# A mixture-of-experts stage with 64 slots per expert, two experts side by side in the array, and float32 gate and up products on raw weights

## Chip, cores, metric

One core of one Trainium2 chip runs the whole program. The metric is the time of one execution in device microseconds (us), the median of several runs.

## What is computed

Two transformer blocks on 256 tokens of width 1024, all in float32. The change touches only the end of the second block, a two-level mixture of experts (4 groups of 4 experts, hidden width 256), and the norm that follows it:

```python
glog = xt @ w_rg + b_rg;  gsel = argmax(glog);  ggate = softmax(glog)[gsel]
elog_g = (xt @ w_re + b_re).reshape(-1, 4, 4)[gsel]      # the chosen group's experts
top_p, top_i = top_k(softmax(elog_g), 2);  top_p /= sum(top_p)
comb = one_hot(4 * gsel + top_i, 16) * (ggate * top_p)    # summed over the two
act = silu(xt @ w1[e]) * (xt @ w3[e]) * comb[:, e]        # gate, up; 1024 -> 256
y = sum over e of act @ w2[e]                             # down; 256 -> 1024
return rmsnorm(x + y)
```

So each token belongs to one group and uses two of that group's four experts. Routed with the reference's inputs of four seeds, the largest group has 83 tokens and the largest expert 54.

## The kernel before, in words

Weights are packed on the host into 134 chunks of 128 x 2048 float32 (1 MiB), in the order of use; the last 48 are the experts': three for each, two of gate and up (each with half of the 1024 input rows, 512 output columns: 256 of gate, 256 of up), one of down. `_emit` (L318) issues a chunk's load on SyncE's queue into a raw buffer and then splits it: ScalarE writes a rounded copy `whi` in the float32r type (L351), VectorE writes the remainder `wlo` (L352). A product in nearly full float32 precision is then three float32r products: hi by hi, hi by lo, lo by hi. The loads are issued in order, each when its raw buffer is free, so SyncE runs ahead as far as buffers allow; `chunk()` (L358) splits one chunk ahead of its use.

`moe_route` (L1689) forms router logits, picks each token's group (`oh`), and ranks the tokens of a group with a triangular product (`rank`); from these come one-hot matrices `Sg` that put the tokens of a group into 128 slots. `moe` (L1731) gathers groups 0 and 1 by a product with `Sg` and splits the result into `ghi`, `glo`; groups 2 and 3 come later by indirect DMA on GpSimd's queue and TensorE transposes. While the first expert is on TensorE, VectorE computes the weights of the experts (`eg`, `ex`, two calls of `first_max`). `facts` (L1807) brings each slot's token number and weights into slot order by small float32 products.

`experts` (L1851) then walks over the 16 experts. For each: 24 float32r products of 512 columns (`ahead`: gate and up for the 128 slots of the group), Silu and multiply (`act`), two transposes and a split (`turn`), and 12 products of 512 columns (`down`) that add to the group's `y`. After a group's fourth expert `finish` (L1928) adds the residual, normalizes, and scatters the rows to the output by indirect DMA. At the very end, a group with over 128 tokens would make a fallback run (L1976).

The list of who multiplies what with float32 operands matters for the change: `values2` (L757, through `pairs`, L746) already puts two products of 64 output rows side by side in the array, with plain float32 operands.

Of the kernel before, what the change touches and what calls it, by code (L numbers as in the profile page):

```python
# [7 lines left out]
F32 = mybir.dt.float32  # L8
# [9 lines left out]
N_CHUNKS = 134  # L18

# [82 lines left out]
def _pack(x):  # L102
# [81 lines left out]
    for e in range(18):  # L184
        if e < 16:
            w13 = np.concatenate([_rows(x["w_exp_gate_2"][0, e]), _rows(x["w_exp_up_2"][0, e])], 2)
            put(w13[:, 0:4])
            put(w13[:, 4:8])
        if e > 1:
            put(_rows(x["w_exp_down_2"][0, e - 2]))  # L190
# [66 lines left out]
class Kernel:  # L257
    def __init__(self, ctx, tc, ins, out, dump=None, stop=None):
# [13 lines left out]
        self.extra = None  # L272
# [20 lines left out]
    def big(self, tag, name, dt=F32):  # L293
        n, bufs = {"nt": (3072, 1), "m": (2048, 2), "rawm": (2048, 6)}[tag]
        return (self.sb if tag == "m" else self.mx).tile([128, n], dt, name=name, tag=tag, bufs=bufs)
# [22 lines left out]
    def _emit(self, i, cols, first=None):  # L318
# [3 lines left out]
        j = i - LATE - (i > EXTRA)  # L322
        tag = "raw" if j < 0 else None if i == EXTRA else RAW_LATE[j % len(RAW_LATE)]
        if tag is None and self.extra:
            raws, self.extra = self.extra, None
        else:
            if tag in (None, "raw"):
                raw = self.wp.tile([128, 2048], F32, name="raw", tag="raw", bufs=self.NRAW)
            else:
                raw = self.big(tag, "raw")  # L330
            raws = [raw[:, 0:1024], raw[:, 1024:2048]]
            if not first and i != 1:
                nc.sync.dma_start(raw[:, :cols], self.ins["W"][i, :, :cols])
        out, c = [], 0
        for step, load, then in first if first else [(1024, None, None)] * (cols // 1024):
# [4 lines left out]
            if c % 1024 == 0:  # L340
                if i >= LATE_M and (2 * i + c // 1024) % 3 == 2:
                    hl = self.big("m", "whilo", F32R)
                    hi, lo = hl[:, 0:1024], hl[:, 1024:2048]
                else:
                    hi = self.wp.tile([128, 1024], F32R, name="whi", tag="whi", bufs=self.NHI)
                    lo = self.wp.tile([128, 1024], F32R, name="wlo", tag="wlo", bufs=self.NHI)
                out.append((hi, lo))
# [1265 lines left out]
    def late_pool(self):  # L1613

        self.mx_ctx.close()
        self.mx = self.mx_ctx.enter_context(self.tc.tile_pool(name="mo", bufs=1))
        self.bufs.update(s=4, t2=2)

    def moe_start(self):
# [7 lines left out]
        self.wr = self.t("s", name="wr")[:, 0:160]  # L1627
# [7 lines left out]
        self.lg = self.t("s", name="lg")[:, 0:40].rearrange("p (a b) -> p a b", a=2)  # L1635

        self.meta = self.t("s", name="meta")[:, 0:48].rearrange("p (a b) -> p a b", a=2)
        nc.gpsimd.memset(self.meta, 1.0)
        nc.gpsimd.tensor_copy(self.meta[:, :, 0], self.con("tok"))
        self.oh = self.t("c", (2, 4), F32R, name="oh")  # L1640
        self.gm = self.t("c", (2, 1), name="gm")
        self.rank = self.t("c", (2, 4), name="rank")
        self.Sg = [self.t("t2", (2, 256), F32R, name="Sg") for _ in range(2)]
# [45 lines left out]
    def moe_route(self):  # L1689
# [28 lines left out]
        nc.vector.tensor_copy(self.rank, pr[:, 0:8].rearrange("p (a b) -> p a b", a=2))  # L1718
        def places(eng, gs):
            for h in range(2):  # L1720
                for gi in gs:
                    eng.tensor_scalar(self.Sg[gi // 2][:, h, 128 * (gi % 2):128 * (gi % 2) + 128], self.con("iota"),
                                      self.rank[:, h, gi:gi + 1], self.oh[:, h, gi:gi + 1].bitcast(F32),
                                      op0=ALU.is_equal, op1=ALU.mult)

        places(nc.vector, (0, 1))
        for i in range(2):
            self.turn_s(2 + i, tp[i])
        places(nc.gpsimd, (2, 3))

    def moe(self):  # L1731
        nc, x = self.nc, self.x
        con, par = self.con, self.par
        thi, tlo = self.thi, self.tlo
        meta = self.meta
        lg, oh, gm, rank, Sg = self.lg, self.oh.bitcast(F32), self.gm, self.rank, self.Sg
        first_max = self.first_max
# [9 lines left out]
        ghi = [self.t("a4", (4, 256), F32R, name="ghi") for _ in range(2)]  # L1747
        glo = [self.t("a4", (4, 256), F32R, name="glo") for _ in range(2)]
        gp = [self.ps("acc", (2, 256)) for _ in range(4)]
        for m, h in [(0, 0), (1, 0), (0, 1), (1, 1)] + [(m, h) for m in range(2, 8) for h in range(2)]:  # L1750
            c = slice(128 * m, 128 * m + 128)
            self.mm(gp[m // 2][:, m % 2], thi[h][:, c], Sg[0][:, h], h == 0 and m % 2 == 0, False,
                    skip_group_check=True)
            self.mm(gp[m // 2][:, m % 2], tlo[h][:, c], Sg[0][:, h], False, h == 1, skip_group_check=True)
        for m in range(8):
            self.split(ghi[m // 4][:, m % 4], glo[m // 4][:, m % 4], gp[m // 2][:, m % 2], par("n2", m))
        hg = [v[:, k] for v in ghi for k in range(4)], [v[:, k] for v in glo for k in range(4)]

        self.extra = [self.t("a4", name="raw") for _ in range(2)]
        for k in range(2):  # L1760
            nc.sync.dma_start(self.extra[k], self.ins["W"][EXTRA, :, 1024 * k:1024 * k + 1024])
# [3 lines left out]
        nc.vector.tensor_tensor(dg, gl, b4(gm), ALU.subtract)  # L1765
        nc.scalar.activation(dg, dg, AF.Exp)
        gs = c3("gs", 1)
        nc.vector.tensor_reduce(gs[:, :, 0], dg, axis=AX.X, op=ALU.add)
        nc.vector.reciprocal(gs, gs)

        eg = c3("eg")
        for gi in range(4):
            el = lg[:, :, 4 + 4 * gi:8 + 4 * gi]
            if gi == 0:
                nc.vector.tensor_tensor(eg, el, b4(oh[:, :, 0:1]), ALU.mult)
            else:
                tmp = c3("tmp")
                nc.vector.tensor_tensor(tmp, el, b4(oh[:, :, gi:gi + 1]), ALU.mult)
                nc.vector.tensor_tensor(eg, eg, tmp, ALU.add)
        em = c3("em", 1)  # L1780
        nc.vector.tensor_reduce(em[:, :, 0], eg, axis=AX.X, op=ALU.max)
        ex = c3("ex")
        nc.vector.tensor_tensor(ex, eg, b4(em), ALU.subtract)
        nc.scalar.activation(ex, ex, AF.Exp)
        warm = self.t("c", name="warm")[:, 0:1]
        nc.scalar.activation(warm, ex[:, 0, 0:1], AF.Silu)
        oh1, oh2 = c3("oh1"), c3("oh2")
        m1, m2 = c3("m1", 1), c3("m2", 1)
        first_max(oh1, ex, m1)
        rest = c3("rest")  # L1790
        nc.vector.scalar_tensor_tensor(rest, oh1, -2.0, ex, op0=ALU.mult, op1=ALU.add)
# [234 lines left out]
```

## Time and profile before

| | |
|---|---|
| runs | 802.88 us median of 3 (802.06 to 804.18) |
| the profiled execution | 801.04 us, span 799.2 us |
| TensorE busy | 770.2 us (96% of the span), 5640 matmuls |
| VectorE, ScalarE, GpSimd busy | 616.7, 452.8, 98.4 us |
| granted TensorE clock | 0.985 of full speed, mean |

The span runs from the first to the last instruction; the rest of the execution's time lies around it. Matmuls overlap in the pipeline: what one costs in a stream is the distance between the starts of two, not its duration.

### The profile page before, as it was taken

The numbers are of one execution on the slowest core, as the hardware profiler recorded it, in microseconds if no ns is written. First come the engines' busy times: TensorE is split into PE (matmuls) and PEld (weight loads), VectorE is DVE, ScalarE is ACT, GpSimd is POOL, SyncE is SP. The second block draws the span as 40 slices with busy tenths as digits, with TensorE's granted clock in tenths as the row PEclk, the third lists the DMA queues.
The fourth block names the chain that finished last, engine by engine and source line by source line (L and its number), as shares of the span: only waits on it lengthen the run. The fifth ranks groups of instructions, "written<-read, shape, count | busy, mean of one in ns | idle before, by whom it ended". The sixth has DMA issues, their size and how long they took to land. (4 is left out here: it accounts for less than half of the span.)

```text
span 799.2 us, 14325 instructions
## 1 busy us (share of the span) xinstructions
PE 770.2 (96%) x5640; PEld 711.2 (89%) x5640; DVE 616.7 (77%) x1163; ACT 452.8 (57%) x751; POOL 98.4 (12%) x99
## 2 busy tenths in 40 slices
PE   8999999999999999999999899999999899999994
PEld 8988889899999999999999779988899887877873
DVE  6677587777666767887877898777497689999995
ACT  7357346645544455755764233555465477888882
POOL 1000002000000000300100644200014412020111
PEclk9999999999999999999999979999999899999998
DMA  8754424555545455454333313431585759989910
GB/s 320 266 205 171 158 60 153 165 204 164 201 166 203 164 202 167 158 210 158 109 107 132 114 59 81 158 102 58 227 353 165 237 224 363 352 311 385 373 67 28
DMA packets 30505, 149.90 MB, mean 188 GB/s; under 512 B 9440, under 2 KB 10464, under 8 KB 13792
## 3 DMA queue, kind: packets, MB, share of 16 engines
q1 hardware_dynamic: 20880, 141.70, 49.9%
q10 hardware_dynamic: 8400, 4.08, 1.8%
q0 software_dynamic: 1152, 3.15, 1.0%
q8 instruction: 46, 0.75, 0.4%
q14 instruction: 27, 0.22, 0.1%
HBM read 146.42 MB, written 3.54 MB: 188 GB/s over the span
## 5 line engine op out<-in xcount | busy, mean ns | idle before, releaser
L352 DVE TENSOR_TENSOR wlo<-raw,whi 128x1024 fp32r<-128x1024 f32 (+1 forms) x237 | 293.6, 1246 | 88.1 <-ACT whi L351 86.0
L351 ACT ACTIVATE whi<-raw 128x1024 fp32r<-128x1024 f32 (+1 forms) x237 | 247.3, 1048 | 172.2 <-PE acc L368 85.8
L368 PE MATMUL acc<-hhi,whi 128*128 128x256 f32 x344 | 100.2, 291 | 0.0
L368 PE MATMUL acc<-hhi,wlo 128*128 128x256 f32 x344 | 99.2, 289 | 0.6 <-DVE wlo L352 0.6
L368 PE MATMUL sm<-hhi,whi 128*128 128x256 f32 x352 | 99.5, 283 | 0.0
L368 PE MATMUL sm<-hlo,whi 128*128 128x256 f32 x352 | 99.4, 282 | 0.0
L368 PE MATMUL sm<-hhi,wlo 128*128 128x256 f32 x352 | 99.0, 281 | 0.0
L368 PE MATMUL acc<-hlo,whi 128*128 128x256 f32 x344 | 98.6, 287 | 0.0
L368 PEld LDWEIGHTS acc<-hhi,wlo 128*128 128x128 f32 x344 | 65.8, 192 | 2.6 <-issue 1.6
L368 PEld LDWEIGHTS acc<-hhi,whi 128*128 128x128 f32 x344 | 65.9, 192 | 1.3 <-issue 0.8
L368 PEld LDWEIGHTS sm<-hhi,wlo 128*128 128x128 f32 x352 | 66.7, 189 | 0.0
L368 PEld LDWEIGHTS acc<-hlo,whi 128*128 128x128 f32 x344 | 65.9, 191 | 0.8 <-issue 0.6
L368 PEld LDWEIGHTS sm<-hlo,whi 128*128 128x128 f32 x352 | 66.2, 188 | 0.0
L368 PEld LDWEIGHTS sm<-hhi,whi 128*128 128x128 f32 x352 | 66.0, 188 | 0.0
L457 POOL TENSOR_TENSOR sqacc<-sqacc,sq 128x256 f32<-128x256 f32 x19 | 16.2, 851 | 331.4 <-ACT sq L456 330.6
L368 PE MATMUL acc<-alo,whi 128*128 128x256 f32 x176 | 49.5, 281 | 0.0
L368 PE MATMUL acc<-ahi,wlo 128*128 128x256 f32 x176 | 49.4, 281 | 0.0
L368 PE MATMUL acc<-ahi,whi 128*128 128x256 f32 x176 | 49.3, 281 | 0.0
L368 PE MATMUL acc<-xhi,wlo 128*128 128x256 f32 x160 | 45.7, 286 | 1.0 <-DVE wlo L352 0.8
L368 PE MATMUL acc<-xhi,whi 128*128 128x256 f32 x160 | 46.2, 289 | 0.0
L368 PE MATMUL acc<-xlo,whi 128*128 128x256 f32 x160 | 45.4, 284 | 0.0
L352 DVE TENSOR_TENSOR whilo<-raw,whilo 128x1024 fp32r<-128x1024 f32 x32 | 39.0, 1219 | 0.4
(504 smaller groups left out, 1888.6 us busy)
## 6 DMA issues: line engine op xcount, KB each, us to landing
raw<-in_W_dram SPq DMA_DIRECT2D x130, 1024.0 KB, 5.0
raw<-in_W_dram SPq DMA_DIRECT2D x5, 512.0 KB, 6.8
raw<-in_W_dram SPq DMA_DIRECT2D x4, 256.0 KB, 4.8
xd<-xr ACTq DMA_DIRECT2D x2, 512.0 KB, 8.2
dec<-in_con_dram ACTq DMA_DIRECT2D x2, 384.0 KB, 4.3
conm<-in_con_dram SPq DMA_DIRECT2D x1, 576.0 KB, 7.0
xa<-in_xT_dram SPq DMA_DIRECT2D x2, 256.0 KB, 4.4
xb<-in_xT_dram SPq DMA_DIRECT2D x2, 256.0 KB, 5.2
```

Of the source, the lines that this page charges most:

```text
L351: nc.scalar.activation(h, r, AF.Copy)
L352: nc.vector.tensor_tensor(l, r, h.bitcast(F32), ALU.subtract)
L368: return self.nc.tensor.matmul(out, a, b, start=start, stop=stop, **kw).ins
L457: (eng or nc.gpsimd).tensor_tensor(acc, acc, sq, ALU.add)
```

## The change

Each expert gets 64 slots of its own, and each two experts of a group form a pair that fills 128 slots. The input of a pair is one float32 tile `X` (1024 x 128 slots, not split). Gate and up of the two experts of a pair run as plain float32 products on the raw chunks, 64 slots each, into the two halves of one PSUM tile. Their chunks are no longer split; a raw buffer is held until TensorE has used it, and the ring of raw buffers grows from 9 to 11. After Silu, a float32 product with a one-hot matrix `E` turns the activations and spreads them from an expert's 64 slots to the group's 128 in one step, once for each expert, in place of the two transposes. Down is as before. The choice of the experts moves from `moe` into `moe_route`, ahead of the ranking. Two pairs' inputs come from the one-hot gather, the other six by indirect DMA and transposes. The fallback runs if a group has over 128 tokens or an expert over 64.

```diff
+MOE = []
+for _n in range(9):
+    MOE += [(_k, 2 * _n + _e) for _k in range(2) for _e in range(2)] if _n < 8 else []
+    MOE += [(2, 2 * _n - 2 + _e) for _e in range(2)] if _n else []
...
     def _emit(self, i, cols, first=None):
+            j = i - LATE
+            raw = self.big((["rawm"] * 6 + ["raw"] * 3 + ["m"] * 2 * (i >= MOE0))[j % 9 if i < MOE0 else (j - 8) % 11],
+                           "raw")
...
+        if i >= MOE0 and MOE[i - MOE0][0] < 2:
+            return raw
...
     def moe_route(self):
-            self.keep_warm(2, self.slt[:, 0], self.thi[0][:, 0:256])
+            self.keep_warm(6, self.slt[:, 0], self.thi[0][:, 0:256])
+        nc.vector.tensor_tensor(by, self.lg[:, :, 4:20].rearrange("p h (g j) -> p h j g", g=4), ohj, ALU.mult)
+        nc.vector.tensor_reduce(eg, by, axis=AX.X, op=ALU.add)
+        nc.vector.tensor_reduce(em[:, :, 0], eg, axis=AX.X, op=ALU.max)
+        nc.vector.tensor_tensor(ex, eg, em.to_broadcast([128, 2, 4]), ALU.subtract)
+        nc.scalar.activation(ex, ex, AF.Exp)
+        self.first_max(oh1, ex, self.m1)
+        nc.vector.scalar_tensor_tensor(rest, oh1, -2.0, ex, op0=ALU.mult, op1=ALU.add)
+        self.first_max(oh2, rest, self.m2)
+        nc.vector.tensor_tensor(sel, oh1, oh2, ALU.add)
+        nc.vector.tensor_tensor(self.oe..., sel..., ohg, ALU.mult)
-        self.mm(pr[:, 0:8], self.slt[:, 0], self.oh, True, False, skip_group_check=True)
-        ranked = self.mm(pr[:, 4:8], self.slt[:, 1], self.oh[:, 0], False, True, skip_group_check=True)
+        for p, v, n in ((pe, self.oe, 16), (pg, self.oh, 4)):
+            self.mm(p, self.slt[:, 0], v, True, False, skip_group_check=True)
+            ranked = self.mm(p[:, n:2 * n], self.slt[:, 1], v[:, 0], False, True, skip_group_check=True)
...
     def moe(self):
+        def rows(idx):                      # indirect DMA of 128 rows of x
+        def turned(row, dst):               # 8 transposes, 2 scaled copies by VectorE
...
+        def gate_up(n, amid):
+            p = self.ps("sm")
+            last = None
+            for k2 in range(2):
+                ch = self.chunk(), self.chunk()
+                for k in range(4):
+                    for e in range(2):
+                        r = slice(64 * e, 64 * e + 64)
+                        with self.tc.issue_after(last) if last else contextlib.nullcontext():
+                            last = mm(p[r], X[n][:, 4 * k2 + k, r], ch[e][:, 512 * k:512 * k + 512], k2 + k == 0,
+                                      k2 == 1 and k == 3, skip_group_check=True)
+                if k2 == 0:
+                    amid()
...
+        def act(n):
+            nc.scalar.activation(sl, p[:, 0:256], AF.Silu, scale=F.mt[:, n, 2:3])
+            nc.vector.scalar_tensor_tensor(a, p[:, 256:512], F.rc[:, n:n + 1], sl, op0=ALU.mult, op1=ALU.mult)
+            nc.gpsimd.tensor_scalar(E, con("iota"), F.place[:, n:n + 1], None, op0=ALU.is_equal)
+        def spread(n):
+            pts = [self.ps("sm", (2, 128)) for _ in range(2)]
+            self.pairs([[(pts[e][:, i], a[rr[e], 128 * i:128 * i + 128], E[rr[e]], True, True) for i in range(2)]
+                        for e in range(2)], skip_group_check=True)
...
+                self.split(ahi, alo, pts[e])
...
     def finish(...):
-                eng = nc.gpsimd if n else nc.vector
-                eng.tensor_tensor(o, o, fng[:, 512 * n:512 * n + 512], ALU.mult)
+                nc.vector.tensor_tensor(o, o, fng[:, 512 * n:512 * n + 512], ALU.mult)
...
+        for n in range(9):
+            if n < 8:
+                gate_up(n, (lambda: spread(n - 1)) if n else (lambda: None))
+            if n == 0:
+                pair_facts()                # 16 small float32 products, 8 pairs
+                for m in range(2, 4):
+                    prow[m] = rows(F.idx[:, 0, m:m + 1])
+                group_facts()               # 8 small float32 products, 4 groups
+            if n < 8:
+                act(n)
+            else:
+                spread(7)
+            if n % 2 == 0 and n < 8:
+                grow[n // 2] = rows(F.idg[:, 0, n // 2:n // 2 + 1])
+            if n and n + 3 < 8:
+                prow[n + 3] = rows(F.idx[:, 0, n + 3:n + 4])
+            if n:
+                prepare(n + 1)              # turned(prow[n + 1], X[n + 1])
+                down(n - 1)                 # 24 float32r products, split chunks
+                if n % 2 == 0:
+                    finish(y, grow[n // 2 - 1], scatter(n // 2 - 1))
...
-        with self.tc.If(reg > 128):          # reg: the largest group
+        with self.tc.If(reg > 128):          # reg: largest group, or twice the largest expert
```

## Rows read from the trace of the kernel before

**Rows 1.** The page's first line, of the whole execution.
```profile
span 799.2 us, 14325 instructions
```
**Rows 2.** Stretches: length, busy PE, PEld, DVE, ACT, POOL (count), clock, DMA share, GB/s.
```profile
636.50:643.60 7.10, 7.09 (x39) 6.85 (x40) 3.12 (x12) 2.17 (x6) 4.02 (x5) 0.63 0.90 290
643.60:788.40 144.80, 142.32 (x643) 114.12 (x642) 137.62 (x210) 114.35 (x153) 18.16 (x10) 1.00 0.74 278
```
**Rows 3.** TensorE in order of time, expert stage: start, length us, tiles, count.
```profile
658.23 0.39 PE L368 MATMUL sm<-whilo,ghi 128*128 128x512 f32 x1
658.46 1.86 PE L368 MATMUL acc<-meta,Sg 128*128 128x24 f32 x16
660.16 0.48 PE L368 MATMUL sm<-whilo,ghi 128*128 128x512 f32 x1
```
**Rows 4.** TensorE in order of time around one call of values2.
```profile
524.06 0.27 PE L368 MATMUL acc<-hlo,whi 128*128 128x256 f32 x1
524.37 0.87 PE L368 MATMUL sm<-pt,bV 128*64 128x256 f32 x8
525.17 0.93 PE L368 MATMUL sm<-bK,bq 64*128 64x128 f32 x8
```
**Rows 5.** The same around four calls of values2 in a row.
```profile
566.71 2.82 PE L368 MATMUL sm<-de,U 128*64 128x256 f32 x32
569.46 0.38 PE L368 MATMUL acc<-hhi,whi 128*128 128x256 f32 x1
```
**Rows 6.** TensorE groups by shape, 480 to 634 us: count, busy us, mean ns.
```profile
L368 PE MATMUL acc<-hhi,wlo 128*128 128x256 f32 x142 | 40.2, 284 | 0.6 <-DVE wlo L352 0.6
L368 PE MATMUL sm<-pt,bV 128*64 128x256 f32 x16 | 2.6, 404 | 0.0
```
**Rows 7.** TensorE in order of time: transposes of gathered rows.
```profile
675.33 0.60 PE L1844 MATMUL sm<-con,row 128*128 128x128 f32 x4
675.68 0.48 PE L368 MATMUL sm<-whi,ghi 128*128 128x512 f32 x1
```
**Rows 8.** TensorE in order of time, ranking; in brackets idle time, releaser.
```profile
636.51 0.59 PE L368 MATMUL sm<-oh,slt 128*128 128x8 f32 x2 [2.57 <-DVE oh L1687]
636.96 1.20 PE L368 MATMUL acc<-thi,slt 128*128 128x256 f32 x4
```
**Rows 9.** The expert choice, all engines in order of time.
```profile
646.51 0.17 DVE L1783 TENSOR_TENSOR ex<-eg,em 128x8 f32<-128x8 f32 x1
...
646.96 0.16 DVE L1681 TENSOR_REDUCE m<-ex 128x2 f32<-128x8 f32 x1 [0.27 <-ACT ex L1784]
```
**Rows 10.** VectorE in order of time: the choice of the second expert.
```profile
649.63 0.17 DVE L1687 TENSOR_TENSOR oh<-e,f 128x8 f32<-128x8 f32 x1
649.83 0.17 DVE L1791 SCALAR_TENSOR_TENSOR rest<-oh,ex 128x8 f32<-128x8 f32 x1
650.03 0.16 DVE L1681 TENSOR_REDUCE m<-rest 128x2 f32<-128x8 f32 x1
650.23 0.36 DVE L1684 SCALAR_TENSOR_TENSOR e<-rest,m,con 128x4 f32<-128x4 f32 x2
```
**Rows 11.** Tile raw, 640 to 800 us: count, duration ns min/median/max, starts; DMA landing.
```profile
L352 DVE TENSOR_TENSOR wlo<-raw,whi x60: 1204/1217/2354, 647.9 to 783.5; 128x1024 fp32r<-128x1024 f32 x60
L333 SPq DMA_DIRECT2D raw<-in_W_dram x35: 327/328/328, 651.7 to 756.8; - x35
...
DMA to landing us min/median/max: 4.7/7.0/8.5
```
**Rows 12.** A stretch with loads queued throughout; columns as in Rows 2.
```profile
720.00:735.00 15.00, 15.00 (x68) 12.13 (x67) 14.52 (x18) 12.58 (x18) 1.29 (x1) 1.00 1.00 412
```
**Rows 13.** The tail in order of time.
```profile
789.46 0.68 DVE L1937 TENSOR_TENSOR row<-row,fng 128x512 f32<-128x512 f32 x1
...
790.38 1.25 POOL L1937 TENSOR_TENSOR row<-row,fng 128x512 f32<-128x512 f32 x1 [10.37 <-ACT acc L1935]
```
**Rows 14.** Line L1824, the indirect row gathers: time to landing.
```profile
DMA to landing us min/median/max: 6.2/6.5/7.0
```

More of the change, by code (lines that the diff above doesn't have):

```diff
@@ L340, in _emit @@
             if c % 1024 == 0:
[L341 to L346, printed above, removed]
+                hi = self.wp.tile([128, 1024], F32R, name="whi", tag="whi", bufs=self.NHI)
+                lo = self.wp.tile([128, 1024], F32R, name="wlo", tag="wlo", bufs=self.NHI)
                 out.append((hi, lo))
@@ L1769, in moe @@
         nc.vector.reciprocal(gs, gs)
[L1771 to L1791, printed above, removed]
-        first_max(oh2, rest, m2)
         den = c3("den", 1)
-        nc.vector.tensor_tensor(den, m1, m2, ALU.add)
+        nc.vector.tensor_tensor(den, self.m1, self.m2, ALU.add)
         nc.vector.reciprocal(den, den)
@@ L1804, in moe @@
         fng = self.t("a4", name="fng")
         nc.scalar.dma_start(fng, self.ins["fng"])
[L1807 to L1817 removed]
+        pc = self.ps("sm", (20,))
@@ L1928, in finish, with down @@
-        def finish(y, fact):
-            _, _, idx, row = fact
+                self.split(ahi, alo, pts[e])
+                P[n].append((ahi, alo))
+        def down(n):
+            nonlocal y
+            if n % 2 == 0:
+                y = [self.ps("acc"), self.ps("acc")]
+            for e in range(2):
+                ahi, alo = P[n][e]
+                first, last = n % 2 + e == 0, n % 2 == 1 and e == 1
+                ch = self.chunk()
+                for k, c2 in ((0, 0), (1, 0), (0, 1), (1, 1)) if last else ((0, 0), (0, 1), (1, 0), (1, 1)):
+                    hi, lo = ch[k]
+                    c = slice(512 * c2, 512 * c2 + 512)
+                    mm(y[c2], ahi[:, k], hi[:, c], first and k == 0, False, skip_group_check=True)
+                    mm(y[c2], ahi[:, k], lo[:, c], False, False, skip_group_check=True)
+                    mm(y[c2], alo[:, k], hi[:, c], False, last and k == 1, skip_group_check=True)
@@ L1931, in finish @@
+        ends = []
+        def finish(y, row, store):
             ss = self.t("c", name="ss")[:, 0:2]
@@ L1941, in finish @@
             nc.vector.tensor_scalar(row[:, 0:624], row[:, 0:624], rr, None, op0=ALU.mult)
-            d = nc.gpsimd.indirect_dma_start(
-                out=self.out, out_offset=bass.IndirectOffsetOnAxis(ap=idx, axis=0), in_=row, in_offset=None,
-                bounds_check=S - 1, oob_is_err=False)
-            for other in ends:
-                self.tc.declare_no_dep(d.ins, other.ins, reason="rows of another group")
-            ends.append(d)
-        known = []
-        def fact(gi):
-            if not known:
-                known.extend(facts([[Sg[g // 2][:, h, 128 * (g % 2):128 * (g % 2) + 128] for h in range(2)]
-                                    for g in range(4)]))
-            return known[gi]
@@ L1957, in moe @@
-        hg2 = [], []
-        def side():
-            for _ in range(3):
-                yield
-            yield from gather([fact(2)[3], fact(3)[3]], hg2)
-        experts([(e, hg if e < 8 else hg2, 128 * (e // 4 % 2), lambda gi=e // 4: fact(gi), e % 4 == 0, e % 4 == 3)
-                 for e in range(16)], self.chunk, side())
-        cnt = self.t("c", name="cnt")[:, 0:1]
-        pc = self.ps("sm")
-        for h in range(2):
-            self.mm(pc[:, 0:4], self.slt[:, 1], self.oh[:, h], h == 0, h == 1)
@@ L1996, with scatter, store @@
-BV_CHUNK = 1 + 14 + 4 + 33 + 4 + 1 + 2 + 2 + 2 + 2 + 2
-LATE = N_CHUNKS - 56
-EXTRA = N_CHUNKS - 48 + 8
-LATE_M = N_CHUNKS - 48
-RAW_LATE = ["rawm"] * 6 + ["raw"] * 3
+            store(row)
+        def scatter(g):
+            def store(row):
+                d = nc.gpsimd.indirect_dma_start(
+                    out=self.out, out_offset=bass.IndirectOffsetOnAxis(ap=F.idg[:, 1, g:g + 1], axis=0), in_=row,
+                    in_offset=None, bounds_check=S - 1, oob_is_err=False)
+                for other in ends:
+                    self.tc.declare_no_dep(d.ins, other.ins, reason="rows of another group")
+                ends.append(d)
+            return store
```

345 lines of the change are left out of this document (171 added, 174 removed).

## The prediction

> **What bounds the kernel now.** I read first the stretches, then TensorE's instructions in order of time at the edges of the stretch that the change touches, then single operations that the new code shares with the old. The span is 799.2 us [rows 1] and the execution 801.04, so 1.84 us lie around the span; the median of the runs, 802.88, is 1.84 us above this execution. The expert stage runs from 643.60, the first gate and up product, to 788.40, the last down product: 144.80 us, of which TensorE is busy 142.32 at full clock (2.4 GHz), VectorE 137.62, and the DMA engines 74% [rows 2]. A 512-column float32r product starts every 0.23 us [rows 3]; 16 x 36 of them make 132.5 us. So TensorE sets the stage's length, with VectorE (the splits, 1.22 us for each half chunk [rows 11]) 5 us behind it and the loads not far: they wait for raw buffers that VectorE frees. What counts is the new TensorE time, and whether VectorE, the loads or the routing ahead of the stage take over as the bound.
>
> **What a plain float32 product costs.** The trace has the form: `values2` puts two products of 64 output rows side by side. Eight heads have one 256-column product each, and the trace has 16 records [rows 6]: a product leaves two. One such record lasts 404 ns, a float32r one 284 [rows 6]; the 120 ns between are about one more passage of 256 columns (107 ns at 2.4 GHz). So a float32 product passes its columns four times, against three for the split products.
>
> Do the two halves overlap? One call makes 8 records, 4 of 256 and 4 of 128 columns; with two passages each that is 3072 columns, 1.28 us one after the other, 0.64 side by side. From start to next start it took 0.80 us [rows 4]. Four calls in a row would need 2.56 side by side and 5.12 one after the other; they took 2.75 [rows 5]. The excess is 0.16 us in the short run and 0.19 in the long one, so it belongs to the run's edges, not to the work: the halves overlap fully. The Trainium skill has less (TensorE: Matmul & The Clock Gate, Part 3, measured speedup): three column tiles with 512 columns reach 2.38 times, 79% of ideal, and by that the gate and up products would take 69 us, an estimate. The trace differs from it, 0.19 us in 2.75.
>
> At the edges, the step into side-by-side mode takes 0.31 us from the start of a 256-column float32r product that itself passes in 0.11 [rows 4], and the run's own excess is 0.16: some 0.18 us for each change of mode. I take 0.2; bounds 0 and 0.31.
>
> **The new expert stage on TensorE,** from the first gate and up product to the last down product:
>
> - Gate and up: 8 pairs x 8 input tiles x 4 passages x 512 columns / 2.4 GHz (213 ns) = 54.6 us, in place of 384 products at 0.23 = 88.3. The other bound is no overlap, 109.2.
> - Down: unchanged, 192 x 0.23 = 44.2 us.
> - Spread: 4 products of 128 columns for each pair, two at a time in the two halves of the rows: 2 x 4 x 53 ns = 0.43 us, x 8 = 3.4.
> - Transposes of gathered rows: 48 instead of 16; four take 0.35 us [rows 7]: 12 x 0.35 = 4.2.
> - Facts: 24 small float32 products, 48 records, instead of 16 records that took 1.70 us (658.46 to 660.16 [rows 3]): 48 x 0.106 = 5.1. The counting products, moved here from the tail: 4 x 0.11 = 0.4.
> - Changes of mode: into and out of the spread in the middle of gate and up, out to transposes and down, back: 4 for each pair, 32 x 0.2 = 6.4 (0 to 9.9).
> - Waits: the first pair's facts, activation and spread form a chain (Silu, one-hot on GpSimd behind two indirect issues), and the last spread waits for its split. I allow 2 us (0 to 10, see the first rival).
>
> Sum 120.3 us, against 144.8: 24.5 less.
>
> **Does something else become the bound?** VectorE loses the splits of 32 of 48 chunks: 90 half-chunk splits (the 60 of [rows 11] and 30 into a second tile) become 32, 58 x 1.22 = 71 us less; it gains 12 scaled copies of 512 columns (0.7 us each, as a 512-column operation in the tail [rows 13]) and the facts' small operations. About 137.6 - 71 + 12 = 79 us of 120: not the bound, and this is the cover under which all the evacuations lie. The gain of the splits' removal itself is thus nothing; it only makes room. GpSimd gets the one-hots and six more gathers; a gather lands 6.2 to 7.0 us after issue [rows 14] and is issued about an iteration (14 us) ahead.
>
> Loads: 11 chunks fit the ring before the stage begins, 37 must follow. The first two buffers come free 3.4 us into the stage, when TensorE has used them, where before they came free after the split. With loads queued the rate is 412 GB/s [rows 12], 2.55 us for a chunk: 37 x 2.55 = 94 us, ended some 22 us before the stage does. A pair takes 14.2 us on TensorE (6.8 gate and up, 0.4 spread, 0.7 transposes, 5.5 down, 0.8 modes) and 6 x 2.55 = 15.3 us of loading, so the lead of 11 chunks, 28 us of loading, is eaten at 1.1 us a pair and suffices.
>
> **Ahead of the stage.** The choice of the experts moves in front of the ranking, where TensorE already waits 2.57 us for `oh` [rows 8]. Dependent small VectorE operations start 0.20 us apart [rows 10]; subtract and exponential with the hop to ScalarE take 0.45 [rows 9]. Three operations to `em` 0.6, the exponential 0.45, `first_max` 1.0 (five operations, the two `e` together 0.4), twice, and `rest`, `sel`, `oe` 0.6: 3.65 us. Two more ranking products at 0.22 [rows 8]: 0.45. Behind it stand the gather and everything after: +4.1 us. The lower bound is 3.6; as the upper I take 8, since the old chain of one `first_max` needed most of the 2.57 us wait, twice what the spacing of [rows 10] gives. The clock, at 0.63 on average in the 7.10 us after that wait [rows 2], I take as unchanged: it is at half already; at worst as much again is lost, 2.6 us.
>
> **Tail.** The second half's multiplication goes from GpSimd (1.25 us, beside other work) to VectorE (0.68 [rows 13], in line): I take 0.
>
> Net: 24.5 - 4.1 = 20.4 us. 801.04 - 20.4 = 780.6, and 1.84 more for the median: **782.5 us**.
>
> **Rivals.**
>
> 1. *A late split in every pair.* The second down chunk's split stands on VectorE behind the activation and the copies of the transposes; if TensorE waits for one half chunk each time, 8 x 1.22 = 9.8: 792. For it: down follows the transposes by 0.7 us; against: VectorE has a third of its time free. 0.10.
> 2. *Long routing.* The chain takes 8 us and the clock stays half for longer: 3.9 + 2.6 = 6.5: 789. 0.05.
> 3. *Loads set the pace.* In this stage 34 intervals from 651.7 to 756.8 [rows 11] are 3.09 us each. Held to that, the last chunk lands at 651.1 + 36 x 3.09 + 7.0 = 769; split, 12 products and the tail of 10.8 us add 16: 785 where I forecast 778.8: 789. Against it: the loads waited for buffers then. 0.05.
> 4. *Partial overlap,* as if the 0.16 us excess in 0.64 [rows 4] grew with the work: 25% on 54.6 = 13.7 more: 796. The four calls in a row [rows 5] speak against it. 0.05. The Trainium skill's 79%, cited above, would come out at about the same time.
> 5. *Slower: no overlap at 512 columns.* The trace has the halves only at 256 and fewer columns, with small operands. If two raw chunks streamed at 512 columns go one after the other, gate and up take 109.2: +54.6: 837. It decides from 20.4 / 54.6 = 37% of the overlap lost. 0.07.
> 6. *The fallback runs:* 96 more loads, 245 us. Excluded by the counts, largest group 83, largest expert 54.
>
> **Numbers.** The forecast has 0.60, its own range is 776 to 788 (modes 0 to 9.9, waits 0 to 6); a gain beyond that has 0.03. The last 0.05 go to mixtures, such as a third of the overlap lost: 0.03 within 0.3% of before (2.4 us, about what a measurement of this kernel can tell from no change), 0.02 slower. The range 774 to 797 holds the forecast and rivals 1 to 4 (0.85), of which a little may still leave it: 8 in 10. Slower: rival 5 and the 0.02, together 0.09. Same: 0.03. Faster: the rest, 0.88.
>
> **What will show it.** A stage from first gate and up to last down product of some 120 us; gate and up records in twos, 0.43 us apart; VectorE near 65% in the stage; the idle time before the ranking at some 6 us; the loads ended well before the last down product. I am wrong if the records of a pair stand one behind the other, if TensorE idles before `ahi` or `wlo` in every pair, or if the clock falls within gate and up.

## The result and the profile after

The changed kernel takes 790.41 us (median of 4 runs, 788.69 to 793.36) against 803.53 for the kernel before beside it (4 runs): a ratio of 0.9839, 95% interval 0.9802 to 0.9876. It is faster by 1.6%, clear of the noise: 13.1 us where I had forecast 20.4. 790.4 lies in the wide range of 774 to 797, but outside the 776 to 788 that I had given the forecast itself. A second set of five runs gave 793.52 (788.57 to 794.89), ratio 0.9889 (0.9873 to 0.9905). The profiled execution took 790.64 us, span 788.8, which is 10.4 less than the 799.2 of [rows 1].

The page of the changed kernel, its first rows:

```profile
span 788.8 us, 14118 instructions
PE 755.3 (96%) x5616; PEld 669.9 (85%) x5616; DVE 550.6 (70%) x1119; ACT 381.6 (48%) x671; POOL 102.9 (13%) x113
```

Four stretches tell where the time went: from the last product of the projection ahead of the router to the ranking, from there to the first gate and up product, from that to the first down product, and to the end of the last. Columns as in [rows 2]; the last row is the whole expert stage:

```profile
630.58:643.78 13.20, 7.93 (x46) 7.47 (x44) 10.81 (x43) 3.58 (x10) 3.40 (x5) 0.74 0.66 239
643.78:650.61 6.83, 6.83 (x44) 6.77 (x45) 5.04 (x25) 3.29 (x8) 1.89 (x4) 0.75 0.24 77
650.61:675.87 25.26, 25.26 (x129) 13.45 (x129) 6.26 (x35) 2.53 (x8) 10.46 (x13) 0.86 0.71 254
675.87:778.70 102.83, 100.36 (x483) 56.31 (x481) 61.95 (x104) 41.09 (x63) 15.82 (x13) 1.00 0.86 355
650.61:778.70 128.09, 125.62 (x609) 69.75 (x608) 68.21 (x138) 43.62 (x71) 26.27 (x26) 0.97 0.83 335
```

The 144.8 us of [rows 2] end where the last down product of the kernel before starts:

```profile
788.41 0.40 PE L368 MATMUL acc<-whi,alo 128*128 128x512 f32 x1
```

The 128.1 us end where the last one of the changed kernel ends; it starts at 778.30. Counted to that start the stage is 127.7 us long instead of 144.8, so it gave 17.1 of the 24.5 us expected. It starts at 650.61 instead of 643.60, 7.0 us later where I had 4.1. The tail behind the last start is 0.3 us shorter. -17.1 + 7.0 - 0.3 = -10.4, which is what the spans show. VectorE is busy for 68.2 of 128.1 us, 53%, where I had 79 us and near 65%: it is no longer near the bound.

What I had staked most on is there. One half of a pair's gate and up, as TensorE's timeline has it, and what follows:

```profile
761.20 3.65 PE L369 MATMUL sm<-raw,X 128*64 128x512 f32 x16
766.10 0.49 PE L369 MATMUL sm<-E,ea__8590 64*128 64x128 f32 x4 [1.25 <-DVE ea__8590 L1909]
```

Sixteen records of 512 columns begin and end within 3.65 us, where one lasts 0.6: they start in twos, 0.43 us apart, and two halves of the array work at once. (The second row belongs to the late losses, below.) In the undisturbed pairs one pair follows the other after 14.44 us, forecast 14.2.

Where the rest went shows in three places. First, ahead of the ranking. TensorE's timeline, and VectorE's in the same microseconds:

```profile
632.75 0.61 PE L369 MATMUL sm<-ones,sq 128*128 128x1 f32 x4 [0.65 <-POOL sq L1698]
634.16 1.01 PE L369 MATMUL sm<-ones,sq 128*128 128x1 f32 x4 [0.81 <-DVE sq L1699]
...
643.78 0.39 PE L369 MATMUL sm<-oe,slt 128*128 128x32 f32 x2 [3.81 <-DVE oe L1736]
```

```profile
631.59 0.74 DVE L1471 SCALAR_TENSOR_TENSOR x<-acc,x 128x256 f32<-128x256 f32 x2
632.25 1.52 DVE L353 TENSOR_TENSOR wlo<-raw,whi 128x1024 fp32r<-128x1024 f32 x1
633.70 0.41 DVE L1699 TENSOR_TENSOR sq<-x 128x256 f32<-128x256 f32 x1
```

A split of a down chunk, needed 40 us later, stands on VectorE between the last residual and its square (three more stand before the residual); TensorE waits for the squares. The wait of 3.81 us for `oe` is the new chain (the choice of the experts, from `oh` to `oe`), against 2.57 in [rows 8].

Second, the clock. Between the router and the last down product, three stretches lie at half clock (1.2 GHz, in the column PEclk):

```profile
633.87:640.70 6.83, 5.81 (x26) 5.51 (x26) 4.81 (x28) 2.52 (x9) 1.78 (x3) 0.50 0.62 226
644.11:647.53 3.42, 3.42 (x17) 3.38 (x17) 2.98 (x19) 1.80 (x4) 0.00 (x0) 0.50 0.00 0
661.18:668.01 6.83, 6.83 (x26) 4.56 (x27) 3.21 (x22) 0.47 (x1) 1.62 (x2) 0.50 0.69 291
681.65:755.57 73.92, 72.72 (x362) 39.31 (x361) 42.01 (x72) 26.47 (x42) 11.65 (x10) 1.00 1.02 419
```

The kernel before had one there, which reached 5.2 us into the ranking and the gather:

```profile
634.88:641.71 6.83, 5.20 (x23) 4.96 (x24) 3.50 (x13) 1.42 (x5) 5.57 (x8) 0.50 0.99 324
```

The third falls into the facts and the second pair's gate and up:

```profile
657.63 3.81 PE L369 MATMUL acc<-ms,Se 128*128 128x20 f32 x32
661.27 3.58 PE L369 MATMUL acc<-ms,Sg 128*128 128x20 f32 x16
664.78 6.09 PE L369 MATMUL sm<-raw,X 128*64 128x512 f32 x18
```

Sixteen records of the groups' facts take as long as the 32 of the pairs' before them. The fourth row of the windows shows something else: from 681.65 to 755.57 the DMA engines are busy without a pause, at 419 GB/s.

Third, the end. VectorE ahead of the sixth pair's down, and ScalarE at the last activation:

```profile
747.90 0.69 DVE L1863 TENSOR_TENSOR X<-sm,par 128x512 f32<-128x512 f32 x1 [2.99 <-PE sm L1862]
748.51 2.35 DVE L353 TENSOR_TENSOR wlo<-raw,whi 128x1024 fp32r<-128x1024 f32 x2
```

```profile
764.97 0.47 ACT L1907 ACTIVATE sl<-sm,mtp 128x256 f32<-128x256 f32 x1 [3.20 <-PE sm L369]
765.34 2.00 ACT L352 ACTIVATE whi<-raw 128x1024 fp32r<-128x1024 f32 x2
```

VectorE stands idle for 2.99 us before a copy of `X` that waits for a transpose, with two splits queued behind it whose rounded halves ScalarE had finished at 746.3; TensorE then waits 1.0 us for them. ScalarE idles 3.20 us before the last Silu, with the splits of four chunks behind it, the first of which had landed at 756.7.

### The profile page after: what moved, and what is told of

The parts are those of the page before. It is cut to its first block, busy times and chain, and to the rows that moved or that the text cites. A ratio compares the mean times of both kernels' runs of the same rounds, so it can differ in the third digit from the quotient of the medians.

```text
span 788.8 us, 14118 instructions
## 1 busy us (share of the span) xinstructions
PE 755.3 (96%) x5616; PEld 669.9 (85%) x5616; DVE 550.6 (70%) x1119; ACT 381.6 (48%) x671; POOL 102.9 (13%) x113
## 5 line engine op out<-in xcount | busy, mean ns | idle before, releaser
L353 DVE TENSOR_TENSOR wlo<-raw,whi 128x1024 fp32r<-128x1024 f32 (+1 forms) x205 | 252.3, 1240 | 91.6 <-ACT whi L352 89.9
L352 ACT ACTIVATE whi<-raw 128x1024 fp32r<-128x1024 f32 (+1 forms) x205 | 213.0, 1047 | 164.5 <-PE acc L369 84.0
L369 PE MATMUL sm<-hhi,whi 128*128 128x256 f32 x352 | 99.5, 283 | 0.0
L369 PE MATMUL sm<-raw,X 128*64 128x512 f32 x256 | 61.7, 612 | 0.0
L369 PEld LDWEIGHTS sm<-raw,X 128*64 128x64 f32 x256 | 17.8, 140 | 33.0 <-issue 30.3
```

The costliest lines, as they stand in the source:

```text
L352: nc.scalar.activation(h, r, AF.Copy)
L353: nc.vector.tensor_tensor(l, r, h.bitcast(F32), ALU.subtract)
L369: return self.nc.tensor.matmul(out, a, b, start=start, stop=stop, **kw).ins
```

## The experiments

Executions of one kernel differ by up to 6 us here: in the profile of the run named "facts apart" below, TensorE ran 6.8 us at half clock in the middle of the program, far from the change (558.95 to 565.78), and reached the router 4.6 us later than in the yardstick's. So the stretches decide. The first from the last projection product to the ranking, the second on to the first down product, the third to the end of the last; half clock counts from the router to the first down product; us:

| kernel | to ranking | to first down | to the end | half clock | median (runs) | ratio, 95% interval |
|---|---|---|---|---|---|---|
| changed | 13.20 | 32.10 | 102.83 | 17.1 | 790.41 (4) | 0.9839 (0.9802 to 0.9876) |
| changed, yardstick | 13.20 | 31.99 | 102.82 | 17.1 | 793.52 (5) | 0.9889 (0.9873 to 0.9905) |
| facts apart | 12.67 | 31.31 | 102.82 | 17.1 | 790.43 (6) | 0.9855 (0.9832 to 0.9877) |
| short choice | 12.60 | 32.30 | 102.82 | 17.1 | 789.98 (5) | 0.9849 (0.9831 to 0.9867) |
| earlier splits | 13.20 | 31.91 | 101.77 | 17.1 | 789.54 (5) | 0.9853 (0.9833 to 0.9874) |
| held splits | 10.91 | 33.03 | 110.54 | 20.5 | 796.63 (5) | 0.9906 (0.9874 to 0.9939) |
| facts in between | 13.19 | 30.64 | 102.19 | 13.7 | 789.95 (4) | 0.9834 (0.9797 to 0.9871) |
| filled idle time | 13.22 | 30.69 | 104.37 | 13.7 | 788.23 (4) | 0.9813 (0.9781 to 0.9845) |
| order of the last pairs | 13.20 | 33.40 | 99.46 | 20.5 | 786.67 (4) | 0.9795 (0.9764 to 0.9827) |
| four together | 12.64 | 28.65 | 99.47 | 6.8 | 782.92 (5) | 0.9762 (0.9746 to 0.9777) |
| and held splits | 10.02 | 28.65 | 103.73 | 3.4 | 784.75 (5) | 0.9784 (0.9770 to 0.9799) |
| no alternating | 13.20 | 38.97 | 126.19 | 23.9 | 818.92 (1) | |
| splits put back | 26.34 | 32.47 | 124.81 | 30.7 | 825.88 (1) | |

**The yardstick.** No edit.

> The changed kernel once more, as the yardstick for the three runs beside it. Both theories: 790 us, a ratio of 0.98 to the kernel before, the stage from 650 to 778 us with a second stretch of half clock in the small products of the facts.

The stage is there, from 650.18 to 776.62, and the median is 793.5. But here the half clock lay over the whole gather (641.81 to 648.64) and only 3.4 us of it in the facts: the stretches moved, their sum is the same.

**No alternating.**

```diff
-                for k in range(4):
-                    for e in range(2):
+                for e in range(2):
+                    for k in range(4):
```

> Within each half of gate and up the four products of the first expert come first and then the four of the second, where the changed kernel alternates; the same products, loads and buffers. Theory (two records run side by side only when neighbours in the queue stand in different halves of the array, so the second expert rides free): a half pair takes 6.8 us instead of 3.4 to 3.6, the eight pairs 52 to 55 us more, of which the late waits of 3 us hide a part: 835 to 845 us, slower than the kernel before. Rival (TensorE finds the other half's work further back in its queue, or 512 columns cost less than two passages for another reason): under 800 us.

A half pair on TensorE's timeline:

```profile
704.54 5.42 PE L369 MATMUL sm<-raw,X 128*64 128x512 f32 x16
```

And the view of single tiles, from 704.5 to 706.2 and from 706.2 to 707.7 (records that reach into the stretch; shortest, median and longest, first and last start):

```profile
L369 PE MATMUL sm<-raw,X x4: 592/592/644, 704.5 to 705.9; 128*64 128x512 f32 x4
...
L369 PE MATMUL sm<-raw,X x9: 592/592/644, 705.9 to 707.7; 128*64 128x512 f32 x9
```

5.35 us to the next instruction's start, where the changed kernel needs 3.58, and one after the other would need 6.9 (16 x 0.43): +28 us instead of +52. The direction is the theory's, the size is between it and its rival (818.9 us, where the theory had 835 to 845 and the rival under 800): the first four records start alone, 0.43 us apart; then eight more within 1.4 us (the ninth is the fourth again), in twos. So four of the second expert's records start beside the last four of the first's, and its other four again alone. Alternating is what makes the whole overlap.

**Splits put back.**

```diff
-        if i >= MOE0 and MOE[i - MOE0][0] < 2:
-            return raw
...
-        return out
+        return raw if i >= MOE0 and MOE[i - MOE0][0] < 2 else out
```

> The gate and up chunks are split as the kernel before split them, on ScalarE and VectorE; the split halves are not used, the products stay on the raw chunks. Theory (TensorE's gain needs the cover that the dropped splits make): a pair then has 12 half-chunk splits at 1.14 us on VectorE and 3 us of other work, 16.7 us against TensorE's 14.4, and raw buffers come free later: the stage is 10 to 25 us longer, 800 to 815 us, no gain over the kernel before. Rival (VectorE has room for them): 788 to 794 us.

825.9, slower than the kernel before and above the theory's 800 to 815. The stage from the first gate and up product, and the stretch ahead of the ranking:

```profile
630.41:656.76 26.35, 8.27 (x46) 7.83 (x44) 25.98 (x57) 15.47 (x23) 4.74 (x6) 0.63 0.20 73
...
663.96:814.04 150.08, 136.68 (x609) 74.44 (x608) 119.84 (x186) 89.81 (x121) 37.32 (x26) 0.92 0.73 286
```

The stage is 22 us longer, within the theory's 10 to 25. But the theory had VectorE full, and it is busy for 119.8 of 150.1 us. TensorE is idle for 13.4 us instead of 2.5, and much of the rest is the clock: behind the first down product it fell three more times, for 17.1 us together (0.92 in the stage, 0.97 in the changed kernel). 13 us more I had not thought of: splits of the chunks that are loaded ahead stand in the chain of the choice, and VectorE is busy for 25.98 of the 26.35 us that the ranking waits. In this one execution, TensorE's saving is worth something only because the splits are gone.

**Held splits.** (The first down chunks' splits go behind the copies of `X`.)

```diff
+            with contextlib.ExitStack() as held:
+                for ins in self.hold if MOE0 + 8 <= i < MOE0 + 10 else ():
+                    held.enter_context(self.tc.issue_after(ins))
                 nc.scalar.activation(h, r, AF.Copy)
                 nc.vector.tensor_tensor(l, r, h.bitcast(F32), ALU.subtract)
...
+        self.hold = dve.ins, act_.ins
```

> The splits of the first two down chunks (four half chunks) are held behind the copies of X on ScalarE and VectorE, so they no longer stand ahead of the last residuals and squares before the router. Theory (they delay the squares that TensorE waits for): the waits of 0.65 and 0.81 us in the sums of squares go, and from the last product of the projection to the ranking it takes 1.5 to 1.9 us less; the splits are done before the first down, which is 8 us behind the stage's first half pair. Rival (the squares are late for another reason, their own chain of copies, or the held splits are late for the first down): 0 us.

The squares come without a wait, and the ranking still waits for the choice:

```profile
633.20 1.05 PE L372 MATMUL sm<-ones,sq 128*128 128x1 f32 x8
...
642.62 0.60 PE L372 MATMUL sm<-oe,slt 128*128 128x32 f32 x2 [3.80 <-DVE oe L1739]
```

10.91 us instead of 13.20: the four splits cost 2.3 us here, a little more than the theory had. What remains over the 7.17 of the kernel before, 3.74, is the net cost of the chain. But the end took 7.7 us more, all of it between the starts of the sixth and of the eighth pair. TensorE around the sixth pair's gate and up, and the stretch ahead of the ranking:

```profile
729.96 1.09 PE L1866 MATMUL sm<-con,row 128*128 128x128 f32 x8
...
736.20 0.72 PE L372 MATMUL acc<-whi,ahi 128*128 128x512 f32 x2 [1.57 <-ACT whi L355]
```

```profile
631.70:642.62 10.92, 7.12 (x46) 6.76 (x44) 8.56 (x41) 2.52 (x9) 3.39 (x5) 0.62 0.25 97
```

The order on TensorE is another (transposes stand between gate and up products), down waits for rounded halves, and 3.4 us of half clock lie there. Besides, a chunk whose split is held keeps its raw buffer: ahead of the ranking the DMA engines move 97 GB/s x 10.9 us = 1.1 MB, where they moved 239 x 13.2 = 3.2, so two chunks come later from there on. How much of the 7.7 us each of these costs was not separated.

**Short choice.**

```diff
-        self.first_max(oh1, ex, self.m1)
-        nc.vector.scalar_tensor_tensor(rest, oh1, -2.0, ex, op0=ALU.mult, op1=ALU.add)
+        self.first_max(oh1, eg, self.m1)
+        nc.vector.scalar_tensor_tensor(rest, oh1, -10000.0, eg, op0=ALU.mult, op1=ALU.add)
...
```

> The two experts are picked on the logits themselves; maximum, subtraction and exponential leave the chain ahead of the ranking and run beside it. Theory (each dependent small operation of the chain is paid in full, as TensorE waits for its end): from the logits to the ranking 5.5 us instead of 6.8, the stage starts 1.3 us earlier and the execution ends 1 to 1.3 us earlier. Rival (the ranking waits for the evacuations and transposes beside it, or the loads give the time back): under 0.3 us.

0.6 us instead of 1.3: in part. VectorE in the chain, and GpSimd beside it:

```profile
637.53 1.33 DVE L1688 SCALAR_TENSOR_TENSOR e<-eg,m,con 128x4 f32<-128x4 f32 x2
...
639.58 0.65 DVE L1728 SCALAR_TENSOR_TENSOR rest<-oh,eg 128x8 f32<-128x8 f32 x1
...
640.46 0.36 DVE L1688 SCALAR_TENSOR_TENSOR e<-rest,m,con 128x4 f32<-128x4 f32 x2
```

```profile
637.43 2.78 POOL L1670 TENSOR_TENSOR tlo<-xr,thi 128x256 fp32r<-128x256 f32 x4 [6.23 <-ACT thi L1669]
```

The same two operations take 1.33 us while GpSimd forms `tlo`, and 0.36 behind it. `rest`, which takes 0.17 us behind GpSimd's work in the changed kernel, now takes 0.65 beside it: the shorter chain lies under that work longer. The Trainium skill (SBUF — State Buffer, "SBUF: two separate sides") says that a VectorE operation with two operands in SBUF and a GpSimd operation share one pair of ports and shut each other out; these rows agree with it.

**Facts apart.**

```diff
-                group_facts()
...
+            if n == 1:
+                group_facts()
```

> The facts of the groups (8 small float32 products) are formed a pair later, behind the second pair's gate and up; nothing else moves. Theory (the clock falls in the second stretch because 7 us of small products stand there without a break): the 32 records of the pairs' facts alone do not bring the clock down, the 16 records of the groups' facts take 1.7 us instead of 3.5, the second pair's first products start 0.43 us apart instead of 0.85; the second pair's down ends 4 us earlier, the execution is 3 to 4 us shorter than the changed kernel. Rival A (the clock falls because of what stands before the facts, the idle times and short products at the stage's start): the half clock comes as before at about 661 us and covers gate and up of the second pair, 0 us. Rival B (the loads set the end): TensorE gains 4 us at the second pair and idles for them again before the last downs, 0 to 1 us.

(The gather of the first group's rows, which needs these facts, moves with them.) Neither theory nor rival A quite. The clock fell all the same, at 664.76, behind the pairs' facts, and covered the second pair's first products (18 records in 6.2 us, 6.1 in the changed kernel), but only for 3.4 us; ahead of the stage it was down for 13.7 us at a stretch. The groups' facts did take less, 1.8 us. The sum of half clock is that of the changed kernel. The total does not tell the run from the changed kernel. So the clock fell with the pairs' facts alone; the groups' facts behind them were not what brought it down.

**Facts in between.**

```diff
+                    if k2 == 0 and n < 2 and k < 4 - 2 * n:
...
+                            F.pm, last = gen.send(last)
```

> The 48 records of the facts are put between the first pairs' gate and up products, four products at a time, so that no stretch of small products is longer than about 1 us; six more changes of mode. Theory (it is the stretch of small products that brings the half clock within the stage): no half clock after the first gate and up product; from that product to the first down 22 us instead of 23.6 to 25.3. Rival (the half clock in the stage follows from the idle time and the small products ahead of the stage): there is one stretch of half clock in the stage as before, 23.5 to 25.5 us.

The window from the first gate and up product to the first down:

```profile
653.47:675.89 22.42, 22.42 (x129) 11.06 (x129) 6.54 (x35) 2.52 (x8) 6.11 (x8) 1.00 0.64 247
```

Full clock throughout, 22.4 us instead of 25.3, although the small products stand in six places instead of one, with a change of mode on either side of each. The theory holds: with the same small products, in eights between gate and up records, the clock does not fall. The other traces agree: in all ten of the runs in the table that leave the pairs' facts together the clock falls 10 to 13 us behind the first gate and up product, in none of the three that put them in between.

**Filled idle time.**

```diff
-            self.keep_warm(6, self.slt[:, 0], self.thi[0][:, 0:256])
+            self.keep_warm(24, self.slt[:, 0], self.thi[0][:, 0:256])
```

> 18 more products of 256 columns on data that is there fill TensorE's 3.8 us of idle time ahead of the ranking; their result is not used. Theory (the second stretch of half clock, from 641.8 or 644.1 us, is the answer to that idle time): it does not come, the gather's 32 products take 3.8 instead of 5.2 to 6.8 us, the execution is 1.5 to 3 us shorter. Rival (the half clock is brought on by what TensorE did before the idle time, or the added products delay the ranking): the stretch comes all the same, or the ranking starts up to 0.5 us later; 0 us or slower by up to 0.5.

From the ranking to the first gate and up product, then two stretches at half clock later:

```profile
641.89:647.27 5.38, 5.38 (x44) 5.24 (x44) 4.70 (x26) 3.09 (x8) 0.30 (x1) 1.00 0.12 24
659.11:665.94 6.83, 6.83 (x21) 2.85 (x22) 3.47 (x23) 0.00 (x0) 3.84 (x4) 0.50 0.78 291
764.92:768.34 3.42, 3.42 (x10) 2.66 (x9) 3.42 (x5) 3.02 (x4) 0.00 (x0) 0.50 0.00 0
```

The second half clock is gone, and from the ranking to the first gate and up product it takes 5.38 instead of 6.83 (8.37 in the yardstick); the ranking is not later. The third remains in the facts. Another came within the last downs and cost 1.5 us.

**Earlier splits.**

```diff
+        self.AHEAD = 2
```

> The splits of a down chunk are emitted one chunk earlier in the expert stage, so that in the last two pairs they stand ahead of the copies of X and of the last activations in VectorE's queue; the loads and all else keep their order. Theory (the late loss is VectorE's order: splits of chunks that have landed stand behind copies that wait for TensorE): the down of the sixth pair takes 5.8 instead of 7.5 us, the last pair's part shrinks by 1 to 3 us, together 2 to 4 us. Rival (the chunks land too late, the loads set the end): the same time within 1 us, with waits for the landing in place of waits for VectorE.

1.05 us: below the theory's 2 to 4. The order changed only behind the first copy of `X`; the splits for the sixth pair's first chunk still stood behind it.

**Order of the last pairs.** (With the line above; the copies of `X` likewise.)

```diff
+                    for ins in self.behind if n > 5 else ():
+                        behind.enter_context(self.tc.issue_after(ins))
                     act(n)
```

> In the last two pairs, the splits of the two down chunks are put ahead of the activation and of the copies of X on both engines; the loads and their order stay. Theory (the late loss is the order on VectorE and ScalarE, as the chunks land 3 to 6 us before they are needed): the down of the sixth pair takes 5.8 instead of 7.5 us, the seventh runs during the last activation, and from the first down to the last it takes 99.5 to 100.5 instead of 102.8 us. Rival (the chunks land too late, the loads set the end): the splits wait for the landing, the activation behind them is late, 102 to 104 us.

```profile
675.40:774.86 99.46, 98.99 (x483) 56.14 (x480) 62.48 (x104) 41.16 (x64) 16.57 (x13) 1.00 0.88 363
```

```profile
759.13 3.88 ACT L352 ACTIVATE whi<-raw 128x1024 fp32r<-128x1024 f32 x4
762.92 0.45 ACT L1909 ACTIVATE sl<-sm,mtp 128x256 f32<-128x256 f32 x1
```

The same loads, and 3.4 us less: the splits are done when the last Silu comes, and the seventh pair's down fills the time of the activation. It was order, not the loads.

**Four together:** the short choice, the facts in between, the filled idle time, the order.

> Four edits together: the choice on the logits, the facts between gate and up products, the filled idle time ahead of the ranking, the order of the last two pairs (with the transposes kept behind gate and up). Theory (the losses stand in different places and add): 0.6 + 1.2 to 2.8 + 1.5 to 3 + 3.4 us less than the changed kernel's 790 to 793, thus 781 to 786 us. Rival (TensorE runs into the loads, which are at full rate from 670 us on, or the half clock turns up in another place, 1.5 to 3.4 us each time): 786 to 789 us.

```profile
629.31:641.95 12.64, 10.43 (x64) 10.06 (x62) 10.80 (x42) 3.48 (x9) 3.42 (x5) 0.73 0.70 250
641.95:647.33 5.38, 5.38 (x45) 5.25 (x45) 4.72 (x28) 3.17 (x9) 0.24 (x1) 1.00 0.07 17
647.33:670.60 23.27, 23.27 (x129) 11.31 (x129) 6.91 (x35) 2.71 (x8) 8.91 (x13) 1.00 0.66 258
670.60:770.07 99.47, 99.00 (x483) 56.13 (x481) 62.50 (x104) 41.00 (x64) 16.96 (x17) 1.00 0.91 375
```

782.92 us: 19.4 below the kernel before in the same session, with the half clock of the kernel before (6.8 us, ahead of the ranking) and no more. It beats both kernels.

**And held splits.** The order is forced from the third pair on.

> As the run before it, and the first down chunks' splits are held behind the copies of X, with the order of splits before activation and copies forced from the third pair on. Theory (2.3 us less ahead of the ranking, and the late loss that the hold alone brought does not come, as it was an order on VectorE and ScalarE): 779 to 784 us, about 2 us less than without the hold. Rival (the loads set the end, or splits forced ahead of the copies wait for chunks that have not landed): no gain over the run without the hold, up to 5 us worse.

```profile
628.91:638.94 10.03, 8.74 (x64) 8.48 (x62) 8.21 (x40) 2.43 (x8) 3.43 (x5) 0.83 0.27 105
```

```profile
738.57 3.65 PE L373 MATMUL sm<-raw,X 128*64 128x512 f32 x14 [0.97 <-DMA raw<-in_W_dram]
```

```profile
741.10 2.01 ACT L355 ACTIVATE whi<-raw 128x1024 fp32r<-128x1024 f32 x2 [6.40 <-DMA raw<-in_W_dram]
```

The rival: from the last projection product to the ranking it takes 2.6 us less, and TensorE and ScalarE then wait for chunks that have not landed (0.97 and 6.40 us here); the end takes 4.3 us more. The hold itself has a part in it: as in the held splits above, 105 GB/s x 10.0 us = 1.1 MB arrive ahead of the ranking, where the run before had 250 x 12.6 = 3.2. Two chunks are 5 us of loading at 412 GB/s, and from 667.6 to 765 the DMA engines are busy for 98% of the time, so they are not made up. What the order forced from the third pair on costs was not separated.

## Why the prediction was right, and what it mis-sized

The mechanism of the gain held. The two halves overlap fully at 512 columns; rival 5 and the partial overlap of rival 4 fall (the Trainium skill's 79% for three tiles, TensorE: Matmul & The Clock Gate, Part 3, is not seen here: 16 records took 3.58 us where full overlap needs 8 x 0.43). VectorE has room, and the run with the splits put back shows that the gain hangs on it. The idle time ahead of the ranking was to be "some 6 us": 0.65 + 0.81 + 3.81 = 5.3. But one of the three signs of being wrong came: the clock fell within gate and up (661.18 to 668.01, the second pair). And that the time lies in the wide range is partly luck: the rivals had widened it, and what took the time is only in part what they priced.

The size was off in four terms; against the profiled execution of before, 10.0 us of the gain were missing. For the first of them, two rows of VectorE, from the kernel before and from the changed one:

```profile
634.37 1.40 DVE L1684 SCALAR_TENSOR_TENSOR e<-lg,gm,con 128x4 f32<-128x4 f32 x2
```

```profile
640.32 1.40 DVE L1688 SCALAR_TENSOR_TENSOR e<-ex,m,con 128x4 f32<-128x4 f32 x2
```

- *Routing, +4.1.* The chain was to cost 3.65 us, and its net cost is 3.74, but the agreement is luck. From `oh` to `oe` VectorE takes 5.4 us (638.32 to 643.72), not 3.65, mostly because two-operand operations beside GpSimd's `tlo` are slow: 1.40 us for the two `e`, 0.36 in [rows 10]. In the kernel before the same wait stood in the choice of the group (the first row), which now ends ahead of `tlo`; so most of what the new chain loses there, the old one gives back. That the two ranking products more did not show (6.83 us from there to the first gate and up, 7.09 before) fits the clock: 3.4 us of the one and 5.2 of the other were at half clock, and at full clock they would come to 5.1 and 4.5, an estimate. And the stretch up to the ranking grew by 6.0: 2.3 are the down splits that moved ahead of the squares (the held splits show it). I had put down the dropped splits as room for evacuations, and not asked which work would use it first.
- *The clock, "unchanged; at worst 2.6".* This is the step that failed most: 17.1 us at half clock instead of 6.8. I had looked for it ahead of the stage only, and 6.83 us of it lie in the stage, where TensorE shows no idle time. The groups' facts took 3.6 us in it and 1.8 at full clock (facts apart); if all the work there halves like that, the stretch costs 3.4 us, an estimate; the run with the facts in between, which has none in the stage, is 2.8 us shorter there, with more changes of mode in it. I had sized the facts at full clock (5.1; 7.2 measured) and the second pair's gate and up as well.
- *Waits, 2.* The late order cost 3.4 (102.8 against 99.5), in one pair and at the end, where rival 1 had it in every pair.
- *A pair, 14.2.* 14.44: eight pairs make 1.9 us. Two halves of gate and up take 3.58 each, the spread 0.65, transposes 0.85, down 5.77, each to the start of the next, changes of mode with them. I had 13.4 for the work without changes, so one of the four costs about 0.25 us, an estimate from this difference, where I had 0.2.

To these comes 1.2 us by which this execution reached the router later than that of before; repeated runs differ by more. The five (2.3, 3.4, 3.4, 1.9, 1.2) make 12.2 - 2 (allowed for waits) = 10.2; what the ranking's products and the tail gave back is 0.7 + 0.3 = 1.0, so 0.8 us stay unassigned.

The loads I had wrong without harm. They were to end 22 us before the last down; the last chunk landed at 764.4, 14 us before. From 670 to 764.5 the DMA engines moved 404 GB/s x 94.5 us = 38.2 MB, of which 32.5 MB (31 chunks) are weights: I had left out the gathered and scattered rows, 5.5 MB, some eleven transfers of 0.52 MB. The gathers show it too:

```profile
row<-xd,idx POOLq DMA_INDIRECT x10, 14.4
```

14.4 us to landing, 6.2 to 7.0 in [rows 14]. In the changed kernel this did not set the end (the order of the last pairs did, with the same loads). Rival 3 shows only in the last run, where the hold had put two chunks off.

## What to carry to other kernels

When a change takes work off an engine that is nearly full, ask what moves into the room: here splits slid ahead of squares that TensorE waited for, and copies ahead of splits that it needed. Before you hold an operation back, ask which buffer it keeps, and which load waits for that buffer. Add up every transfer of a stage, also the small ones, before calling its loads hidden. A stretch of small products, or an idle time, was paid twice here, as the clock fell with it: putting such products between wide ones (25.3 to 22.4 us), or filling the gap with products whose result nobody needs (6.8 to 5.4 us), kept it up. And when a term comes out right, check its parts: two of them can cancel.

## What the hardware showed unexpectedly

- The clock can fall while the trace shows no idle time on TensorE: it went from 2.4 to 1.2 GHz at 661.18, after 3.6 us of small float32 products of 20 columns and 17 us without a gap. The same products in eights between gate and up records left it at 2.4 GHz.
- Without alternating, TensorE started the second half's products 1.8 us after the first half's, while three of the eight records queued ahead of them had not started: 5.35 us for 16 records. The Trainium skill (TensorE: Matmul & The Clock Gate, Part 3, "The mechanism") has products start strictly in order; this trace shows otherwise for two halves of the array.
